# Softmax attention on transposed scores, with a pair of heads in one two-bank tile

## The chip, the core and the metric

The kernel runs on one core of a Trainium2 chip. A core has a matrix engine (PE, with its weight loads in PEld), a vector engine (DVE), a scalar engine for activations (ACT), a general engine (POOL) and a queue that only starts transfers (SP); each takes its instructions in the order of its own queue and waits on the others through semaphores. The metric is the device time of one execution, in microseconds (us), as the median over runs.

## What is computed

The program is two layers of a hybrid transformer on 512 latent and 256 context tokens of width 1024. In each layer a modulated norm and one input projection feed three mixers side by side: centred mean pooling (width 256), gated linear attention (width 256) and softmax attention (width 512). Their outputs are concatenated, projected, added to the residual, and followed by a squared-ReLU MLP. Layer 0 carries both streams; layer 1 carries the latents, and the context only as keys and values. The softmax attention has 8 query heads of 64 channels on 2 key heads:

```python
def gqa_attend(qb, k, v):
    s = jnp.einsum('bqhgd,bkhd->bhgqk', qb, k, preferred_element_type=jnp.float32) * HEAD_DIM ** -0.5
    p = jax.nn.softmax(s, axis=-1)
    return jnp.einsum('bhgqk,bkhd->bqhgd', p.astype(v.dtype), v)
```

A latent query sees 256 context keys and 512 latent keys in one softmax; a context query, in layer 0 only, sees the 256 context keys.

## The kernel before

Activations are kept feature-major (128 features by tokens). A product in single precision is made of passes over a rounded high part and a low rest (names ending in `hi`/`h` and `lo`/`l`); value products, transposes and sums run in full single precision, which PE does as two instructions each.

Per layer the emission goes: first norm and input projection; then the mixing half, in which four generators are advanced one step at a time by the letters of a string (`STEPS`, one for each layer: `g` gated linear attention, `a` the other projections, `m` modulation of later parts, `t` softmax attention, which itself advances `pool_thread`, the pooling mixer); then the output projection (`op`, L291 called from L1087 on) and the MLP. A scheduler then sets the order of each engine's queue from the emitted program. The string is the same in both kernels.

The softmax attention before, by names and lines:

- `k_stack` (L929 to L941) transposes the keys and writes `kh` and `kl`, each with the 64 channels twice, on both halves of the 128 rows.
- `q_stack` (L1022) transposes a pair of heads' queries and stacks high part over low part, `qs`, so that `kh`·`qs` and `kl`·`qs` over 128 rows give a score (L974, L975).
- A unit is a pair of heads and two query tiles of 128; layer 0 has 12 units (the third of each pair is for the context queries, L958 to L966), layer 1 has 8. `softmax_part` writes scores with queries on the rows (`sc`, 128 x 768), takes the row maximum on DVE (L977), and the exponential with its row sum on ACT (L978).
- `value_part` transposes the probabilities tile by tile (four 128 x 128 transposes for each key tile, L992), copies them out (L996 on ACT, L998 on DVE), multiplies by the values with the two heads side by side on the two column halves of PE (L1001), and brings the reciprocal sums, spread over the 64 rows of each head, in by another product (L1008), a copy and two operations (L1012 to L1017). The result goes to `mixh` and `mixl`, the operands of the output projection.

A unit's value part is emitted between the softmax steps of the unit after it. The banks of the accumulation memory are three pools: `psA` (2 tiles of two banks), `psB` (3 of one bank) and `psC` (1). Weight tiles land in `raw` (3 buffers) and are split into `hi` and `lo` (5 each); attention borrows buffers of all three kinds for `p` and `pe`.

## Time and profile before

| what | us |
| --- | --- |
| median of three runs | 1725.98 |
| lowest and highest run | 1724.35, 1727.54 |
| span of the profiled execution (its own total time isn't listed; the median is 6.1 more than the span) | 1719.9 |
| layer 0: keys' copies begin, out-projection begins | 223.3, 387.97 |
| layer 1: keys' copies begin, out-projection begins | 1179.8, 1302.18 |
| PE busy over the span | 1639.1 (95%) |
| DVE, ACT, POOL busy over the span | 866.9, 656.9, 480.3 |

The softmax attention lies in two stretches, about 224 to 387 us and 1180 to 1302 us, where it shares the engines with the gated linear attention and the pooling. The rest of the span is dominated by PE's weight products. Rows of the trace are quoted with their line, engine, operation and tile names; durations in rows are in us unless given as mean ns. PE's matmuls overlap, so what one costs PE is read from the distance between the starts of two rows.

### The profile page before, as it was taken

How to read it: one execution, taken by the hardware profiler on the slowest of the kernel's cores; microseconds unless marked ns; L12 is line 12 of the kernel's file. 1: busy time of each engine (PE TensorE's matmuls, PEld its weight loads, DVE VectorE, ACT ScalarE, POOL GpSimd, SP SyncE). 2: the span in 40 equal slices, each digit the busy share in tenths (PEclk: the TensorE clock that was granted, in tenths of full speed). 3: DMA queues.
4: the chain of work that ended last, by engine and by line, in shares of the span. 5: the costliest groups of instructions: out<-in, count | busy, mean ns of one | idle time of the engine just before them, and what ended most of it. 6: DMA issues, size and time to landing. Idle time of an engine off the chain costs nothing.

```text
span 1719.9 us, 28685 instructions
## 1 busy us (share of the span) xinstructions
PE 1639.1 (95%) x12059; PEld 1337.3 (78%) x12059; DVE 866.9 (50%) x1209; ACT 656.9 (38%) x1136; POOL 480.3 (28%) x514
## 2 busy tenths in 40 slices
...
GB/s 309 131 85 75 136 161 3 100 27 122 111 138 96 153 50 184 120 94 147 50 122 56 68 89 75 72 2 2 2 74 130 79 99 98 99 98 98 98 98 49
DMA packets 140256, 163.38 MB, mean 95 GB/s; under 512 B 9412, under 2 KB 116304, under 8 KB 140128
## 3 DMA queue, kind: packets, MB, share of 16 engines
...
q14 instruction: 34, 0.28, 0.0%
...
## 4 chain that ended last, share of the span: by engine, by line
PE 85%; DVE 5%; POOL 3%; DMA 2%; ACT 2%; issue 2%; SPq 0%; ACTq 0%; POOLq 0%; DVEq 0%
PE dn L291 25%; PE up L272 19%; PE op L291 7%; PE tm L291 6%; PE up L274 5%; PE fm L272 4%; PE av L1001 3%; PE pT L992 2%; PE pm L175 2%; PE up L281 2%; PE fm L274 2%; DMA rawm<-in_w_mod_dram 1%; PE sc L974 1%; PE att L722 1%; PE sc L975 1%
## 5 line engine op out<-in xcount | busy, mean ns | idle before, releaser
L144 ACT ACTIVATE whi<-raw 128x1024 fp32r<-128x1024 f32 (+2 forms) x182 | 184.8, 1031 | 582.2 <-PE dn L291 310.3
L1131 POOL TENSOR_TENSOR X<-X,rtmp 128x512 f32<-128x512 f32 x158 | 218.0, 1384 | 660.9 <-DVE rtmp L1130 660.6
L68 DVE TENSOR_TENSOR wlo<-raw,whi 128x1024 fp32r<-128x1024 f32 (+2 forms) x182 | 225.5, 1247 | 279.0 <-ACT whi L144 273.7
L291 PE MATMUL dn<-whi,ah 128*128 128x512 f32 x640 | 249.8, 390 | 0.4 <-DVE rtmp L1130 0.4
L291 PE MATMUL dn<-whi,al 128*128 128x512 f32 x640 | 249.1, 389 | 0.0
L291 PE MATMUL dn<-wlo,ah 128*128 128x512 f32 x640 | 246.8, 389 | 0.0
L1130 DVE TENSOR_TENSOR rtmp<-dn,ga 128x512 f32<-128x512 f32 x160 | 109.2, 689 | 231.4 <-PE dn L291 229.8
L272 PE MATMUL up<-h2h,whi 128*128 128x512 f32 x464 | 183.8, 396 | 0.7 <-ACT relu L1173 0.7
L272 PE MATMUL up<-h2l,whi 128*128 128x512 f32 x464 | 182.5, 393 | 0.0
L272 PE MATMUL up<-h2h,wlo 128*128 128x512 f32 x464 | 182.5, 393 | 0.0
L291 PEld LDWEIGHTS dn<-whi,ah 128*128 128x128 f32 x640 | 120.1, 188 | 29.8 <-ACT whi L144 4.2
L291 PEld LDWEIGHTS dn<-wlo,ah 128*128 128x128 f32 x640 | 120.1, 188 | 25.0
L291 PEld LDWEIGHTS dn<-whi,al 128*128 128x128 f32 x640 | 120.1, 188 | 24.5
L272 PEld LDWEIGHTS up<-h2h,whi 128*128 128x128 f32 x464 | 87.1, 188 | 31.4 <-ACT relu L1173 7.6
L272 PEld LDWEIGHTS up<-h2l,whi 128*128 128x128 f32 x464 | 87.1, 188 | 21.1 <-issue 1.7
L291 PE MATMUL tm<-whi,hTh 128*128 128x256 f32 (+1 forms) x352 | 102.6, 292 | 0.0
L272 PEld LDWEIGHTS up<-h2h,wlo 128*128 128x128 f32 x464 | 87.1, 188 | 19.6
L291 PE MATMUL tm<-whi,hTl 128*128 128x256 f32 (+1 forms) x352 | 101.3, 288 | 0.0
L291 PE MATMUL tm<-wlo,hTh 128*128 128x256 f32 (+1 forms) x352 | 100.5, 287 | 0.0
L291 PE MATMUL op<-whi,mixh 128*128 128x256 f32 x320 | 91.2, 285 | 0.9 <-ACT whi L144 0.9
L291 PE MATMUL op<-wlo,mixh 128*128 128x256 f32 x320 | 90.2, 284 | 0.3 <-DVE wlo L68 0.3
L291 PE MATMUL op<-whi,mixl 128*128 128x256 f32 x320 | 90.5, 283 | 0.0
...
## 6 DMA issues: line engine op xcount, KB each, us to landing
...
```

Source lines behind the costliest of these rows:

```text
L68: V.tensor_tensor(lo, full, hi.bitcast(F32), ALU.subtract)
L144: A.activation(hi, raw, AF.Copy)
L175: T.matmul(pm[32 * j:32 * j + 32, :], sstat[:, k, :], raw[:, (j % 2) * 512:(j % 2) * 512 + 512], start=(k == 0), stop=(k == KT - 1), skip_ ...
L272: T.matmul(ps[:, 0:NL], a, b[:, 0:NL], start=st, stop=sp_)
L274: T.matmul(ps[:, NL:NT], a, b[:, NL:NT], start=st, stop=sp_)
L281: T.matmul(ps[:, cs], a, b[:, cs], start=(k == 0 and i == 0), stop=(k == nk - 1 and i == 2))
L291: T.matmul(ps, a[:, sl], bb, start=(k == 0 and i == 0), stop=(k == nk - 1 and i == 2))
L722: T.matmul(ps[g * bw:(g + 1) * bw, o0:o0 + bw], xk[rows, j0:j0 + bw], xq[rows, i0:i0 + bw], start=True, stop=True)
L992: T.transpose(pt_[:, i * 128:(i + 1) * 128], p_[:, ki * 128:(ki + 1) * 128], ident)
L1001: T.matmul(av_[64 * hh:64 * hh + 64, 0:256], vst, pe[:, hh * 256:hh * 256 + 256], start=(ki == 0), stop=(ki == len(kts) - 1))
L1130: V.tensor_tensor(tmp, ps, ga[0 if t < 4 else 1][:, sl], ALU.mult)
L1131: (V if b == NB - 1 and not both and t == 3 else G).tensor_tensor(X[t][:, sl], X[t][:, sl], tmp, ALU.add)
```

## The change

The scores are made with the keys on the rows, `sT` (128 keys by 2 heads x 512 queries, two banks), so that the exponential, one instruction of 128 x 1024 for each key tile and pair, yields the operand of the value product directly: the transposes, the copies and the per-query row sums go away. A maximum along the rows no longer exists in this layout, so it is found ahead: `max_part` makes approximate scores of the pair with the queries on the rows (only the product with `kh`; 64 rows for the latent keys), reduces them on DVE to one maximum per query and head, transposes the maxima by a product with an identity, and writes the negated maximum into row 64 of the second query operand `qm`, against a row of ones in row 64 of `kl`. The score's second product then subtracts it. Sums over the keys are made by adding probability tiles (three adds on POOL, two on DVE, for each pair) and one product with ones. `weigh` turns sums into reciprocals by logarithm, exponential and one correction step on DVE. The buffers of the sums, `acc`, are of the `raw` kind. The context queries (`ctx_part`, layer 0) go the same way with 256 columns. `att_thread` emits a pair's values with the maximum of the next pair between them, and two steps of the pooling mixer after each pair.

Lines above the attention move by 5 to 6; L291 becomes L296. The core of the diff:

```diff
     ident = const.tile([128, 128], F32, name="ident")
     make_identity(nc, ident)
+    identr = const.tile([128, 128], F32R, name="identr")
+    V.tensor_copy(identr, ident)
+
+    nmx = const.tile([128, 6, 33], F32R, name="nmx")
+    A.activation(nmx, ident[:, 0:1].unsqueeze(1).to_broadcast([128, 6, 33]), AF.Copy, scale=0.0)
     mhalf = const.tile([128, 1], F32, name="mhalf")
...
@@ -937,129 +943,153 @@
                 A.activation(kh[0:64], src, AF.Copy)
                 sub_lo(kl[0:64], src, kh[0:64])
                 A.activation(kh[64:128], src, AF.Copy)
-                G.tensor_copy(kl[64:128], kl[0:64].bitcast(F32))
+                A.activation(kl[64:65], ident[64:65, 64:65].to_broadcast([1, NT]), AF.Copy)
                 kst.append((kh, kl))
...
-        def q_stack(hp):
+        def max_part(hp):
             mix_new(4 + hp)
             pq = [psB("qT"), psB("qT")] if both else [psB("qT")]
             for t in live:
                 T.transpose(pq[t // 4][:, (t % 4) * 128:(t % 4 + 1) * 128], qview(t, hp), ident)
             for hh in range(2):
-                qs = slot("qs", F32R)
+                qs, qm = slot("qs", F32R), slot("qm", F32R)
+                hr, lr = slice(64 * hh, 64 * hh + 64), slice(64 - 64 * hh, 128 - 64 * hh)
                 for i, pq_ in enumerate(pq):
                     n0, n1 = (0, NL) if i == 0 else (NL, NT)
-                    src = pq_[64 * hh:64 * hh + 64, 0:n1 - n0]
-                    A.activation(qs[0:64, n0:n1], src, AF.Copy)
-                    sub_lo(qs[64:128, n0:n1], src, qs[0:64, n0:n1])
-                qst[hp * 2 + hh] = qs
+                    src = pq_[hr, 0:n1 - n0]
+                    A.activation(qs[hr, n0:n1], src, AF.Copy)
+                    sub_lo(qs[lr, n0:n1], src, qs[hr, n0:n1])
+                G.tensor_copy(qm[0:64, 0:N_], qs[hr, 0:N_].bitcast(F32))
+                qst[2 * hp + hh] = (qs, qm)
+            yield
+            kh = kst[hp // 2][0]
+            parts = mp.tile([128, 2, 6, 2], F32, tag="mxp", name=nm("mxp"), bufs=1)
+            for t in live:
+                ts_ = slice(t * 128, (t + 1) * 128)
+                ps = psB("mxc")
+                for hh in range(2):
+                    T.matmul(ps[:, hh * NC:(hh + 1) * NC], qst[2 * hp + hh][0][:, ts_], kh[:, NL:NT], start=True, stop=True)
+                if t < 4:
+                    pl_ = [psB("mx"), psB("mx")]
+                    for hh in range(2):
+                        hr = slice(64 * hh, 64 * hh + 64)
+                        T.matmul(pl_[hh], qst[2 * hp + hh][0][hr, ts_], kh[hr, 0:NL], start=True, stop=True)
+                V.tensor_reduce(parts[:, 1, t], ps.rearrange("p (h k) -> p h k", h=2), AX.X, ALU.max, negate=True)
+                if t < 4:
+                    for hh in range(2):
+                        V.tensor_reduce(parts[:, 0, t, hh:hh + 1], pl_[hh], AX.X, ALU.max, negate=True)
+                yield
+            V.tensor_tensor(nmx[:, 0:4, 0:33:32], parts[:, 0, 0:4], parts[:, 1, 0:4], ALU.min)
+            if both:
+                V.tensor_copy(nmx[:, 4:6, 0:33:32], parts[:, 1, 4:6])
+            ps = psA("mT")
+            for t in live:
+                T.matmul(ps[0:33, t * 128:(t + 1) * 128], nmx[:, t], identr, start=True, stop=True)
+            for hh in range(2):
+                r0 = 32 * hh
+                A.activation(qst[2 * hp + hh][1][64:65, 0:N_], ps[r0:r0 + 1, 0:N_], AF.Copy)
+            yield
+        def scores(ps, hp, hh, kt, q0, qn):
+            kh, kl = kst[hp // 2]
+            qs, qm = qst[2 * hp + hh]
+            ks = slice(kt * 128, (kt + 1) * 128)
+            T.matmul(ps, kh[:, ks], qs[:, q0:q0 + qn], start=True, stop=False)
+            T.matmul(ps, kl[0:65, ks], qm[0:65, q0:q0 + qn], start=False, stop=True)
+        def weigh(hp, av, acc, q0, n):
+            f = slot("f", w=512)[:, 0:n]
+            A.activation(f, av, AF.Copy)
+            sm = psB("sum")[:, 0:n]
+            for hh in range(2):
+                T.matmul(sm[64 * hh:64 * hh + 64], one.to_broadcast([128, 64]), acc[hh], start=True, stop=True)
+            r, u = slot("r", w=512)[:, 0:n], slot("u", w=512)[:, 0:n]
+            A.activation(r, sm, AF.Ln)
+            A.activation(r, r, AF.Exp, scale=-1.0)
+            V.scalar_tensor_tensor(u, r, -1.0, sm, ALU.mult, ALU.mult)
+            V.tensor_tensor(r, f, r, ALU.mult)
+            V.scalar_tensor_tensor(r, u, 2.0, r, ALU.add, ALU.mult)
+            mhi, mlo = mixT[4 + hp]
+            A.activation(mhi[:, q0:q0 + n], r, AF.Copy)
+            G.tensor_tensor(mlo[:, q0:q0 + n], r, mhi[:, q0:q0 + n].bitcast(F32), ALU.subtract)
+        def lat_part(hp):
+            av = psC("av")
+            P = []
+            def values(kt):
+                for hh in range(2):
+                    T.matmul(av[64 * hh:64 * hh + 64, :], vview(kt, hp // 2), P[kt][:, hh * 512:hh * 512 + 512],
+                             start=(kt == 0), stop=(kt == 5))
+            for kt in range(6):
+                s_ = psA("sT")
+                for hh in range(2):
+                    scores(s_[:, hh * 512:hh * 512 + 512], hp, hh, kt, 0, NL)
+                P.append(wp.tile([128, 1024], F32, tag="lo" if kt % 2 else "hi", name=nm("p")))
+                A.activation(P[kt], s_, AF.Exp)
+                if kt:
+                    values(kt - 1)
+                if kt == 1:
+                    acc = wp.tile([128, 1024], F32, tag="raw", name=nm("acc"), bufs=3)
+                    G.tensor_tensor(acc, P[0], P[1], ALU.add)
+                elif kt in (2, 3):
+                    G.tensor_tensor(acc, acc, P[kt], ALU.add)
+                yield
+            values(5)
+            acc2 = wp.tile([128, 1024], F32, tag="raw", name=nm("acc"), bufs=3)
+            V.tensor_tensor(acc2, P[4], P[5], ALU.add)
+            V.tensor_tensor(acc, acc, acc2, ALU.add)
+            yield
+            weigh(hp, av, [acc[:, 0:512], acc[:, 512:1024]], 0, NL)
+            yield
+        def ctx_part(hp):
+            av = psC("avc")[:, 0:NC]
+            s_ = psA("sTc")
+            for hh in range(2):
+                for i in range(2):
+                    o = i * 512 + hh * NC
+                    scores(s_[:, o:o + NC], hp, hh, 4 + i, NL, NC)
+            p_ = wp.tile([128, 1024], F32, tag="hi", name=nm("p"))
+            A.activation(p_, s_, AF.Exp)
+            yield
+            for i in range(2):
+                for hh in range(2):
+                    o = i * 512 + hh * NC
+                    T.matmul(av[64 * hh:64 * hh + 64, :], vview(4 + i, hp // 2), p_[:, o:o + NC],
+                             start=(i == 0), stop=(i == 1))
+            acc = slot("accx", w=512)
+            G.tensor_tensor(acc, p_[:, 0:512], p_[:, 512:1024], ALU.add)
+            yield
+            weigh(hp, av, [acc[:, 0:NC], acc[:, NC:512]], NL, NC)
+            yield
         def att_thread():
             k_stack()
             yield
-            q_stack(0)
-            yield
-            nonlocal nunits
-            units = [(hp, q0) for hp in range(4) for q0 in ((0, 2, 4) if both else (0, 2))]
-            nunits = len(units)
-            prev = iter(())
-            for n, (hp, q0) in enumerate(units):
-                P = []
-                for i, _ in enumerate(softmax_part(n, hp, q0, P)):
-                    for _ in range(2 if i < 2 else 1):
-                        next(prev, None)
+            yield from max_part(0)
+            for hp in range(4):
+                nxt = max_part(hp + 1) if hp < 3 else iter(())
+                for part in (lat_part(hp), ctx_part(hp) if both else iter(())):
+                    for _ in part:
+                        next(nxt, None)
+                        yield
+                for _ in nxt:
                     yield
-                run(prev)
-                if q0 == 0 and hp < 3:
-                    q_stack(hp + 1)
-                prev = value_part(n, hp, q0, P)
                 next(pool_, None)
-                yield
-            yield from prev
+                next(pool_, None)
             run(pool_)
```

How the queues stand now, at three places. Numbers at the end of a name tell tiles apart.

ACT in layer 0, where the queries of the third pair are copied: `qT` are the transposed queries, `qs` their stacked copies, `p` the probabilities of the second pair. Before:

```order
L1016 ACTIVATE mixh_2671<-f_3388 128x256
L1016 ACTIVATE mixh_2671<-f_3501 128x256
L1033 ACTIVATE qs_3629<-qT_3621 64x512
L1033 ACTIVATE qs_3629<-qT_3622 64x256
L978 ACTIVATE p_3404,sm_3401<-sc_3489,nmx_3402 128x768
L1033 ACTIVATE qs_3634<-qT_3621 64x512
L1033 ACTIVATE qs_3634<-qT_3622 64x256
L978 ACTIVATE p_3405,sm_3401<-sc_3506,nmx_3402 128x768
```

After:

```order
L1037 ACTIVATE p_3627<-sT_3622 128x1024
L964 ACTIVATE qs_3547<-qT_3539 64x512
L964 ACTIVATE qs_3547<-qT_3540 64x256
L1037 ACTIVATE p_3647<-sT_3642 128x1024
L964 ACTIVATE qs_3554<-qT_3539 64x512
L964 ACTIVATE qs_3554<-qT_3540 64x256
L1037 ACTIVATE p_3712<-sT_3707 128x1024
L1037 ACTIVATE p_3731<-sT_3726 128x1024
```

The copies stood among the four exponentials of the first of the second pair's three units, with two more units to come before the third pair's scores; they now stand between the third and the fifth of the second pair's six exponentials. On PE, the third pair's approximate scores (`mxc`, `mx`, which read those `qs`) stand among the second pair's last scores and values (`av`):

```order
L975 MATMUL mxc_3573<-kh_2669,qs_3547 128x256
L1029 MATMUL av_3529<-p_3647,UV_1141 64x512 x2
L1002 MATMUL sT_3726<-qs_2902,kh_2663 128x512
L1003 MATMUL sT_3726<-qm_2903,kl_2664 128x512
L1002 MATMUL sT_3726<-qs_2909,kh_2663 128x512
L1003 MATMUL sT_3726<-qm_2910,kl_2664 128x512
L975 MATMUL mxc_3573<-kh_2669,qs_3554 128x256
L980 MATMUL mx_3576<-kh_2669,qs_3547 128x512
L1029 MATMUL av_3529<-p_3712,UV_1141 64x512 x2
L980 MATMUL mx_3577<-kh_2669,qs_3554 128x512
```

PE in layer 1, around the second half of the pooling mixer (`pool`, from `pm`) before:

```order
L974 MATMUL sc_12049<-kh_11209,qs_11348 128x512
L975 MATMUL sc_12049<-kl_11210,qs_11348 128x512
L974 MATMUL sc_12049<-kh_11209,qs_11348 128x256
L975 MATMUL sc_12049<-kl_11210,qs_11348 128x256
L920 MATMUL pool_12114<-pm_11200,wpl_9588 128x512
L974 MATMUL sc_12125<-kh_11215,qs_11923 128x512
L975 MATMUL sc_12125<-kl_11216,qs_11923 128x512
```

After:

```order
L1011 MATMUL sum_11724<-acc_11514,one 64x512 x2
L957 MATMUL qT_11769<-ident,Uq_10498 128x128 x3
L957 MATMUL qT_11769<-ident,Uq_10725 128x128
L925 MATMUL pool_11754<-pm_10900,wpl_9288 128x512
L1002 MATMUL sT_11760<-qs_11450,kh_10915 128x512
L1003 MATMUL sT_11760<-qm_11451,kl_10916 128x512
L1002 MATMUL sT_11760<-qs_11455,kh_10915 128x512
L1003 MATMUL sT_11760<-qm_11456,kl_10916 128x512
L1002 MATMUL sT_11784<-qs_11450,kh_10915 128x512
```

The pooling product stood between the scores of two units of softmax attention; it now stands ahead of the third pair's first scores, behind the sums (`sum`) of the second pair.

PE in layer 0, where attention ends. Before:

```order
L992 MATMUL pT_4434<-ident,pcx_4371 128x128 x2
L992 MATMUL pT_4434<-ident,pcx_4372 128x128 x2
L1008 MATMUL rb_4443<-ident,sm_4340 64x128 x4
L1001 MATMUL av_4424<-pe_4430,UV_1137 64x256 x2
L1001 MATMUL av_4424<-pe_4439,UV_1137 64x256 x2
L291 MATMUL op_4480<-whi_4470,mixh_3393 128x256
L291 MATMUL op_4480<-whi_4470,mixl_3394 128x256
```

After:

```order
L1002 MATMUL sTc_4122<-qs_3854,kh_2669 128x256
L1003 MATMUL sTc_4122<-qm_3855,kl_2670 128x256
L1002 MATMUL sTc_4122<-qs_3854,kh_2669 128x256
L1003 MATMUL sTc_4122<-qm_3855,kl_2670 128x256
L1011 MATMUL sum_4109<-acc_4062,one 64x512 x2
L1067 MATMUL avc_4121<-p_4131,UV_1141 64x256 x4
L296 MATMUL op_4348<-whi_4338,mixh_3805 128x256
L296 MATMUL op_4348<-whi_4338,mixl_3806 128x256
```

The last row sets of attention were the value products of the context unit (`pcx`); they are now the sums of the last pair and its context values (`avc`). The first output projection in the new queue reads the weight tile `whi_4338`, whose transfer into a `raw` buffer is the third of four on SP's queue for that projection.

70 lines of the change are left out of this document (removed).

## The prediction

> **What bounds the kernel now.** I read the page's list of engines and its chain first, then a view of the two stretches with softmax attention, then single rows there.
>
> ```profile
> PE 1639.1 (95%) x12059; PEld 1337.3 (78%) x12059; DVE 866.9 (50%) x1209; ACT 656.9 (38%) x1136; POOL 480.3 (28%) x514
> PE 85%; DVE 5%; POOL 3%; DMA 2%; ACT 2%; issue 2%; SPq 0%; ACTq 0%; POOLq 0%; DVEq 0%
> core 0: us, PE busy (x) PEld busy (x) DVE busy (x) ACT busy (x) POOL busy (x), PEclk, DMA share, GB/s
> 224.00:386.70 162.70, 145.39 (x1740) 95.97 (x1735) 103.77 (x169) 102.07 (x230) 55.29 (x74) 0.96 0.18 63
> 1180.00:1302.20 122.20, 108.77 (x1215) 73.24 (x1213) 82.72 (x131) 81.83 (x174) 38.83 (x55) 0.94 0.12 44
> 262.00:290.00 28.00, 21.91 (x500) 15.40 (x500) 24.96 (x38) 17.28 (x40) 17.04 (x25) 0.88 0.01 3
> 1186.00:1215.00 29.00, 23.34 (x341) 16.31 (x341) 26.31 (x40) 22.40 (x52) 22.29 (x33) 0.82 0.01 2
> 320.00:387.00 67.00, 63.54 (x470) 41.96 (x469) 35.35 (x58) 44.95 (x107) 12.54 (x19) 1.00 0.22 81
> ```
>
> PE is the bound over the whole, and the change touches only the 163 and 122 us of the two stretches; what comes behind them keeps its order and its time. Inside, two regimes: at the start of each stretch DVE is busy for 24.96 of 28 and 26.31 of 29 us and PE has holes, towards the end PE is busy for 63.54 of 67. Work taken from PE pays only in the second regime; work given to DVE costs in the first.
>
> **What the change does to each engine.** The distances between starts give what a piece costs PE:
>
> ```profile
> 325.87 1.08 PE L1001 MATMUL av<-pe,UV 128*64 128x256 f32 x8
> 326.88 0.66 PE L992 MATMUL pT<-ident,p 128*128 128x128 f32 x4
> 327.47 0.65 PE L1001 MATMUL av<-pe,UV 128*64 128x256 f32 x4
> 328.06 0.66 PE L992 MATMUL pT<-ident,p 128*128 128x128 f32 x4
> 331.45 0.47 PE L974 MATMUL sc<-kh,qs 128*128 128x512 f32 x1
> 331.77 0.39 PE L975 MATMUL sc<-kl,qs 128*128 128x512 f32 x1
> 331.99 0.28 PE L974 MATMUL sc<-kh,qs 128*128 128x256 f32 x1
> 332.11 0.28 PE L975 MATMUL sc<-kl,qs 128*128 128x256 f32 x1
> 332.23 0.38 PE L992 MATMUL pT<-ident,pcx 128*128 128x128 f32 x2
> ```
>
> Four transposes take 0.59 (326.88 to 327.47), a key tile's four value instructions 0.59, eight in a row 1.01; so 0.43 for four more without a switch. A score instruction of 512 columns takes 0.22, or 0.32 behind full-precision work, one of 256 takes 0.12. A pair in layer 0 costs before: scores 8 x 0.78 = 6.2 and 1.0 for the context, transposes 14 x 0.59 = 8.3, values 14 x 0.58 = 8.1, sums about 1.3: 24.9. After: scores 24 x 0.22 + 6 x 0.1 = 5.9 and 1.1, approximate scores 8 x 0.22 + 12 x 0.12 = 3.2, transposed maxima about 0.7, values 6 x 1.0 + 1.2 = 7.2 (512 columns: 0.86 and a switch of 0.15), sums 1.6: 19.7. Layer 1 by the same prices: 20.9 and 16.4. PE saves 4 x 5.2 + 4 x 4.5 = 39.
>
> ```profile
> L977 DVE TENSOR_REDUCE nmx<-sc 128x1 f32<-128x768 f32 x64 | 60.5, 953 | 25.9 <-PE sc L975 25.5
> L962 DVE TENSOR_REDUCE nmx<-scc 128x4 f32<-128x1024 f32 x4 | 4.9, 1223 | 2.0 <-PE scc L961 1.9
> L978 ACT ACTIVATE p<-sc,nmx 128x768 f32<-128x768 f32 x64 | 57.5, 899 | 18.7 <-DVE nmx L977 18.1
> L1173 ACT ACTIVATE relu<-up 128x768 f32<-128x768 f32 x32 | 25.6, 800 | 71.6 <-PE up L274 55.6 <-DMA brow<-in_b_mod_dram 14.4 <-PE up L281 1.6
> L1173 ACT ACTIVATE relu<-up 128x512 f32<-128x512 f32 x32 | 18.6, 581 | 0.0
> L68 DVE TENSOR_TENSOR wlo<-raw,whi 128x1024 fp32r<-128x1024 f32 x170 | 213.9, 1266 | 273.5 <-ACT whi L144 268.5 <-PE pm L175 2.3 <-ACT pe L996 1.9
> L1131 POOL TENSOR_TENSOR X<-X,rtmp 128x512 f32<-128x512 f32 x158 | 218.0, 1384 | 660.9 <-DVE rtmp L1130 660.6
> L699 DVE TENSOR_TENSOR xq<-xq,gq 128x768 f32<-128x768 f32 x14 | 16.8, 1209 | 0.8 <-ACT xq L698 0.7
> L1130 DVE TENSOR_TENSOR rtmp<-dn,ga 128x512 f32<-128x512 f32 x160 | 109.2, 689 | 231.4 <-PE dn L291 229.8
> L68 DVE TENSOR_TENSOR qs<-qT,qs 64x512 fp32r<-64x512 f32 x16 | 11.0, 690 | 2.9 <-ACT qs L1033 2.3
> L1014 DVE TENSOR_TENSOR f<-av,f 128x256 f32<-128x256 f32 x20 | 8.4, 418 | 12.1 <-ACT pe L996 6.1 <-PE av L1001 5.3 <-ACT f L1012 0.6
> L1017 POOL TENSOR_TENSOR mixl<-f,mixh 128x256 fp32r<-128x256 f32 x20 | 16.5, 823 | 115.6 <-ACT mixh L1016 115.5
> L913 POOL TENSOR_TENSOR pl<-pl,edge 64x8 f32<-64x8 f32 x12 | 5.2, 436 | 19.7 <-DVE pl L910 12.1 <-DVE pl L905 3.1 <-DVE pl L907 2.9
> L915 DVE SCALAR_TENSOR_TENSOR pm<-pl,invw,pl 64x512 f32<-64x512 f32 x8 | 6.1, 758 | 0.4 <-POOL pl L914 0.3
> ```
>
> A reduction of 512 columns is not in the trace; 1.223 - 0.953 for 256 columns gives 0.953 - 0.27 = 0.69 (bounds 0.61, half the largest row, and 0.953). An exponential of 1024 columns is 0.899 and the 0.22 that 256 columns cost between the two L1173 rows, 1.12 (bounds 1.02, by those rows alone, and 1.20, by the 768 row in proportion). An add of 128 x 1024 is 1.27 on DVE (the `wlo` row) and 2 x 1.384 = 2.77 on POOL. So DVE has per pair in layer 0: 14 reductions 9.7, adds 2.5, corrections 3 x 0.69 + 3 x 0.42 = 3.3, query rests 2 x (0.69 + 0.42) = 2.2, together 17.7, 71 over the layer. Before, a pair has 8 x 0.953, 1.2, the same rests, four copies of about 0.69 and three products of 0.418, 15.0 and some small ones, about 63 over the layer. POOL gains three adds, 8.3, a context add of 1.4 and two casts, about 11 per pair. ACT loses the copies and most row sums. No engine then fills its stretch: PE 145 - 21 = 124 of 163, DVE 112, POOL about 100.
>
> **The chain that sets the end.** With no engine full, the order of the queues decides. Call m0 to m3 the times at which DVE has a pair's maxima; scores of a pair wait for them, since the negated maximum rides in their second product. What the queue order (shown with the change) makes of it, link by link:
>
> ```profile
> L937 ACT ACTIVATE kh<-kT x4: 803/805/807, 223.3 to 1182.4; 64x768 fp32r<-64x768 f32 x4
> L782 PE MATMUL rg<-ident,rsg x80: 272/273/476, 247.9 to 1255.0; 128*64 128x128 f32 x80
> L920 PE MATMUL pool<-pm,wpl 128*128 128x512 f32 x8 | 4.5, 628 | 0.4 <-issue 0.2 <-DVE dg L735 0.2
> 381.82 3.76 DMA raw<-in_w_out_dram
> 385.60 1.06 ACT whi L144
> 386.69 1.24 DVE wlo L68
> 387.97 7.10 PE op L291 x57
> 1302.18 2.59 PE op L291 x20
> ```
>
> Layer 0. The first approximate scores stand on PE behind the product `rg`, which ran from 247.9, so DVE begins about 250; ahead of m0 it has 13 reductions (9.0), nine products of gated attention like the L699 row (9 x 1.25 = 11.3) and a copy or two: m0 = 271. To m1: DVE 13 reductions, four products, query rests, masks and two `qe` products, about 21, PE about 27 with the gated attention's small products: +26. To m2: adds 2.5, sums 1, logarithm, exponential and context exponential 3, context scores and values with small products about 6; then six key tiles at 2.0 on PE (scores 1.0, values 1.0), 12; the third pair's query copies stand on ACT behind the third and fourth of these exponentials, so 11 of 14 reductions come after, 7.6, with adds, gated attention's scaling and its wait, 5: +37 (31 to 43, by how much of the last 12 overlaps the tiles). To m3 the same without the small products: 5.5 + 12 + 12.5 and about 2 of wait: +32. To the out-projection: 4.8 for the maxima's row, the context unit and a pooling product ahead of the tiles, 12 for these, adds and sum 5.3; then the transfer of the weight tile that its first rows read, which lands in a `raw` buffer that `acc` holds until the sum has read it, by the rows above 3.76 + 1.06: +27. 271 + 26 + 37 + 32 + 27 = 393 against 387.97: +5, range -1 to +11.
>
> Layer 1. Keys at 1180; DVE has 12 reductions (8.3), products and states, about 21: m0 = 1201. Then +25 and +23 by the same counts with four tiles. To m3: adds 2.5, sum and reciprocal 2.4, weighing 2.1; then the pooling chain, whose product the queue puts ahead of the third pair's first scores: a copy to `mixh` 0.6, POOL's rest (0.823 for 256 columns, about 1.4 here) and copy 0.8, four DVE rows of 0.69, POOL's four edge products of at most 0.436, 1.4, two rows of 0.758, the product 0.63, about 9 with the hand-offs; then 12 for tiles and about 8 for the reductions left over: +36 (33 to 39). PE has nothing to do in those 9. To the out-projection the maxima's row 1.7, tiles 12, the last exponential 1.1, adds 2.5 and the sum 0.5: +18. 1201 + 25 + 23 + 36 + 18 = 1303 against 1302.18: +1, range -4 to +8.
>
> Hand-offs between engines are left out so far. The rows at 385.60 to 387.97 show 0.03 and 0.04 for one, the L977 row shows 25.9 / 64 = 0.4; some 70 of them on the chain cost 2 to 28, and I take 0.1, 7. Total: +5 + 1 + 7 = +13. 1719.9 + 13 = 1733, and with the 6.1 by which the median stood over the span, **1739**. With the ends of the three terms, 1723 to 1773; all far ends together are unlikely, so its own range is 1726 to 1757.
>
> **A rule against the change.** POOL's adds read and write the same memory as DVE's. The `xq` row took 1.209 for 768 columns beside POOL's work, 1.57 ns a column, the `wlo` row 1.24. In the Trainium skill, "SBUF — State Buffer", section "SBUF: two separate sides", DVE with two operands from that memory and POOL exclude each other for a whole instruction. By that rule a DVE add or product could wait out one POOL add, 24 x 2.77 / 2 = 33 more by estimate, 1772. The trace's 1.57 against 1.24 is far less than a full exclusion, so it is not in my sum; the ratio itself is used in the last rival.
>
> **Rivals.**
>
> *Overlap works, PE stays the bound or DVE fills the stretch.* For it: 63.54 of 67 us busy at the end of layer 0, and the emission puts a pair's maxima between the tiles of the pair before. Against: the copies' place on ACT and the serial links above. All of PE's saving, -39, gives 1726 - 39 = 1687.
>
> *Only part overlaps.* If the reductions counted behind the tiles on the way to m2 and m3 in layer 0 and to m3 in layer 1, 8 each, hide beneath them: 1739 - 24 = 1715. For it: three banks in `psB` let PE run one reduction ahead. Against: those copies again, and adds of 2.77 on POOL ahead of the `qm` casts that the pair needs.
>
> *Stalls and saving cancel,* about 1726: the chain without hand-offs, -7, and with the low end of layer 0, -6.
>
> *Clock and shared memory make it slower still.* Where PE has holes the granted clock was 0.88 and 0.82, where it is dense 1.00. The change puts holes through both stretches: PE's 124 and 91 us there at 0.85 instead of 0.95 are 215 x 0.12 = 25 more, half of it on the chain, 13; POOL's 24 adds at the 1.57 / 1.24 ratio give 24 x 0.7 = 17, half on the chain, 8: 1739 + 21 = 1760. It decides from a mean clock below about 0.88 in both stretches. The Trainium skill, "TensorE: Matmul & The Clock Gate", section "Part 1: The HAM clock gate", says that the clock halves after an idle window of about 3.4 us; the hole of 9 us in layer 1 would do it, and the rows at 0.82 and 0.88 agree in direction.
>
> **How the numbers follow.** A measurement of this kernel tells 0.2%, 3.5 us, from no change. The chain as forecast, slower by 1730 to 1757: 0.42. Beyond 1757 by clock and memory: 0.08. Cancelled, 1722.5 to 1729.5: 0.12. Part overlap, 1702 to 1722: 0.22. Full overlap, 1675 to 1702: 0.16. So faster 0.38, same 0.12, slower 0.50. The range leaves out about 0.1 at each end: 1693 to 1758; the forecast's own range stands above.
>
> **What would show it.** Right: PE's busy time over both stretches together down by 35 to 40 with spans no shorter; PE waiting for `nmx`, `qm` or `pool` ahead of `sT`, 9 us at one place in layer 1; idle time of DVE's reductions ended by `mx` and `mxc` behind the tiles; out-projections starting near 393 to 400 and, from a layer-1 start that is as much later, 122 to 129 after the keys; a last transfer of `raw` on layer 0's chain. Wrong: reductions that run between the key tiles in all pairs, or an exponential or a 512-column value product well off 1.12 and 1.0, the two prices that the tile of 2.0 rests on. If PE's slots came out above 2.5 the saving itself would be gone.

## The result, and the profile after

| | before | after | forecast |
| --- | --- | --- | --- |
| median of the runs, us | 1725.88 | 1788.66 (1787.81 to 1789.55) | 1739 (1693 to 1758) |
| ratio to before, 95% interval | | 1.0382 (1.0361 to 1.0403) | 1.008 |
| span of the profiled execution | 1719.9 | 1787.0 | 1733 |
| layer 0, first copy of the keys to first out-projection | 163.4 | 194.0 | 170 |
| first out-projection to layer 1's keys | 793.1 | 800.2 | |
| layer 1, first copy of the keys to first out-projection | 122.3 | 148.2 | 123 |
| from there to the end | 417.8 | 421.5 | |

The change made the kernel 63 us slower. The direction was forecast, the size was not: the time lies outside the range. Of the span's 67.1 us, 30.6 lie in the stretch of layer 0, 25.9 in that of layer 1, and 10.8 behind the two, where no instruction had been changed. The profiled execution of the changed kernel lies 2.2 us under its own time (1787.0 of 1789.17), that of the kernel before 6.1 under its median, so it was probably some 4 us quicker than that median, and the spans differ by that much more than the medians, which are 62.8 apart.

The page of the changed kernel, its list of engines and the granted clock in 40 slices:

```profile
PE 1660.6 (93%) x11459; PEld 1311.7 (73%) x11459; DVE 904.3 (51%) x1238; ACT 631.7 (35%) x985; POOL 547.0 (31%) x546
PEclk9999877888999999999999999897788999999999
```

PE has 600 instructions fewer than before (11459 against 12059) and is busy for 21.5 us longer. The two stretches tell why. The windows view of the changed kernel (start and end, length, busy time and instructions of PE, PEld, DVE, ACT, POOL, then granted clock, DMA share, GB/s):

```profile
223.10:417.10 194.00, 159.10 (x1432) 82.55 (x1430) 134.18 (x189) 89.11 (x138) 89.60 (x90) 0.82 0.18 59
1217.30:1365.50 148.20, 112.66 (x932) 57.40 (x930) 86.06 (x136) 67.02 (x108) 68.42 (x69) 0.80 0.07 26
```

The clock fell from 0.96 and 0.94 to 0.82 and 0.80, and no engine is full: PE has 35 idle us in each stretch, DVE 60 and 62. This is the chain of hand-offs that was forecast, and longer than forecast. The same view, cut where DVE has finished the maxima of each pair (its row L986, 268.7 to 1346.6), that is at m0 to m3 and, in layer 0, at the out-projection:

```profile
223.10:268.70 45.60, 35.66 (x270) 18.71 (x268) 29.96 (x51) 18.24 (x30) 23.63 (x22) 0.76 0.36 114
268.70:297.30 28.60, 26.08 (x444) 14.43 (x446) 21.31 (x31) 15.05 (x26) 14.45 (x13) 0.67 0.01 2
297.30:347.40 50.10, 43.40 (x512) 25.10 (x510) 32.97 (x53) 21.11 (x37) 18.78 (x24) 0.88 0.03 6
347.40:385.60 38.20, 29.99 (x110) 14.06 (x108) 31.55 (x37) 16.21 (x24) 18.28 (x17) 0.81 0.26 104
385.60:417.10 31.50, 23.97 (x102) 10.25 (x98) 18.38 (x21) 18.49 (x24) 14.47 (x15) 0.93 0.20 61
1217.00:1237.10 20.10, 14.06 (x76) 8.03 (x74) 16.11 (x28) 9.93 (x15) 7.38 (x12) 0.65 0.00 1
1237.10:1268.40 31.30, 25.23 (x188) 13.02 (x188) 17.44 (x30) 16.96 (x33) 19.29 (x19) 0.83 0.00 1
1268.40:1302.80 34.40, 24.74 (x453) 14.11 (x454) 21.29 (x39) 14.56 (x26) 16.33 (x18) 0.77 0.01 2
1302.80:1346.60 43.80, 31.92 (x165) 15.54 (x163) 25.66 (x37) 15.21 (x22) 17.10 (x17) 0.88 0.09 35
```

The links against the forecast: layer 0 gave m0 = 268.7 (271), then +28.6 (+26), +50.1 (+37), +38.2 (+32), +31.5 (+27). Layer 1 gave +19.8 from the keys (+21), then +31.3 (+25), +34.4 (+23), +43.8 (+36), +18.9 (+18). Only two links lie within 2 us; the largest misses are m1 to m2 in both layers.

The prices of single instructions on ACT, DVE and POOL were not the cause. The groups of the changed kernel (busy us, mean ns of one, then the idle time ahead of them and what ended it):

```profile
L1037 ACT ACTIVATE p<-sT 128x1024 f32<-128x1024 f32 x48 | 48.9, 1023 | 37.7 <-PE sT L1003 37.5
L984 DVE TENSOR_REDUCE mxp<-mx 128x1 f32<-128x512 f32 x64 | 42.1, 681 | 6.4 <-PE mx L980 6.2
L981 DVE TENSOR_REDUCE mxp<-mxc 128x2 f32<-128x512 f32 x40 | 27.2, 682 | 12.9 <-PE mxc L975 12.9
L1044 POOL TENSOR_TENSOR acc<-acc,p 128x1024 f32<-128x1024 f32 x16 | 38.5, 2404 | 11.2 <-ACT p L1037 10.6
```

The exponential took 1.02 us (forecast 1.12), a reduction 0.68 (0.69), an add on POOL 2.40 (2.77). What failed is how they stand to each other.

**The third pair of layer 0,** with the fourth pair's maxima, shows the chain. On PE, from m2 at 347.4 (start, duration, line, operation and tiles; in brackets the idle time ahead and what ended it):

```profile
353.87 0.58 PE L1002 MATMUL sT<-qs,kh 128*128 128x512 f32 x1
...
374.11 0.58 PE L975 MATMUL mxc<-kh,qs 128*128 128x256 f32 x1 [5.10 <-DVE qs L68]
...
380.50 0.79 PE L980 MATMUL mx<-kh,qs 64*128 64x512 f32 x1 [0.46 <-DVE mxp L984]
```

First scores 6.5 us after m2, six key tiles until 369.0, then 5.1 us in which PE waits for the fourth pair's query rests, then all approximate scores in a row from 374.1, in step with DVE's reductions, until 385.6. Of the fourth pair's approximate scores, which had been emitted between the tiles, a single product (`mxc`, at 367.61) ran ahead of the last values. Over both layers 36 of the 104 reductions began between the first and the last exponential of some pair's six tiles. Six tiles with none of them there took 11.9 to 12.9 us from the first exponential to the last, those with eight to twelve of them 17.0 to 24.1. Products of the gated attention stand there as well, and six tiles with these and only two reductions took 17.3, so the reductions are not all of the difference. Why the rests were late stands on DVE:

```profile
362.81 2.87 DVE L910 TENSOR_TENSOR pl<-pl 128x526 f32<-128x526 f32 x1 [0.51 <-POOL pl L909]
...
366.87 0.68 DVE L68 TENSOR_TENSOR qs<-qT,qs 64x512 fp32r<-64x512 f32 x1
367.59 2.80 DVE L915 TENSOR_TENSOR pl<-pl 128x520 f32<-128x520 f32 x1
```

and beside it on POOL:

```profile
362.75 2.37 POOL L1044 TENSOR_TENSOR acc<-acc,p 128x1024 f32<-128x1024 f32 x1
...
367.49 2.34 POOL L1044 TENSOR_TENSOR acc<-acc,p 128x1024 f32<-128x1024 f32 x1
```

A pooling add of 526 columns, which takes 0.71 at this place when POOL has no such add (e1, below), took 2.87: it started 0.06 us behind POOL's add and ended 0.56 after it. L915 repeats this: it ended 0.56 after an add that had started 0.10 earlier. By these lengths the pooling mixer and the query rests behind it lost some 4 us here.

**From m1 to m2 in layer 0** another chain stands among the maxima, the scaling of the gated attention (`ss`, `rsg`, `rg`):

```profile
309.42 0.50 PE L1002 MATMUL sT<-qs,kh 128*128 128x512 f32 x1
...
331.04 0.50 PE L980 MATMUL mx<-kh,qs 64*128 64x512 f32 x1
331.47 0.51 PE L975 MATMUL mxc<-kh,qs 128*128 128x256 f32 x2
331.90 1.08 PE L1029 MATMUL av<-p,UV 128*64 128x512 f32 x4
...
337.09 2.72 PE L776 MATMUL ss<-blk,o 128*128 128x2 f32 x12
341.30 2.83 PE L787 MATMUL rg<-ident,rsg 128*64 128x128 f32 x24 [1.50 <-DVE rsg L223]
344.06 0.80 PE L975 MATMUL mxc<-kh,qs 128*128 128x256 f32 x2
```

Between 337.09 and 344.06 no approximate score runs. The same 24 `rg` took 1.53 in the kernel before:

```profile
314.84 1.53 PE L782 MATMUL rg<-ident,rsg 128*64 128x128 f32 x24
```

**In layer 1** three waits stand out on PE:

```profile
1268.60 1.97 PE L1011 MATMUL sum<-acc,one 128*64 128x512 f32 x4 [4.09 <-DVE nmx L986]
...
1283.58 2.05 PE L925 MATMUL pool<-pm,wpl 128*128 128x512 f32 x2 [8.74 <-DVE pm L920]
...
1321.61 2.04 PE L925 MATMUL pool<-pm,wpl 128*128 128x512 f32 x2 [10.61 <-DVE pm L920]
```

The last was in the forecast, with 9; the one of 8.74, the first half of the pooling mixer ahead of the second pair's first scores, was not.

**Behind the stretch** of layer 0 the first out-projections run at a low clock:

```profile
417.12 0.39 PE L296 MATMUL op<-whi,mixh 128*128 128x256 f32 x1 [1.87 <-ACT whi L149]
...
419.62 0.41 PE L296 MATMUL op<-whi,mixh 128*128 128x256 f32 x1
419.83 0.41 PE L296 MATMUL op<-whi,mixl 128*128 128x256 f32 x1
...
426.01 0.28 PE L296 MATMUL op<-whi,mixh 128*128 128x256 f32 x1
426.13 0.28 PE L296 MATMUL op<-whi,mixl 128*128 128x256 f32 x1
```

From start to start 0.21, and 0.12 from 424.3 on; about 3.5 us are lost, at work that the change does not touch.

### The profile page after: what moved, and what is told of

It reads as the page before. It is cut to its first block, busy times and chain, and to the rows that moved or that the text cites. A ratio compares the mean times of both kernels' runs of the same rounds, so it can differ in the third digit from the quotient of the medians.

```text
span 1787.0 us, 27365 instructions
## 1 busy us (share of the span) xinstructions
PE 1660.6 (93%) x11459; PEld 1311.7 (73%) x11459; DVE 904.3 (51%) x1238; ACT 631.7 (35%) x985; POOL 547.0 (31%) x546
## 5 line engine op out<-in xcount | busy, mean ns | idle before, releaser
L296 PE MATMUL dn<-whi,ah 128*128 128x512 f32 x640 | 249.8, 390 | 0.4 <-DVE rtmp L1160 0.4
L296 PE MATMUL dn<-whi,al 128*128 128x512 f32 x640 | 249.1, 389 | 0.0
L296 PE MATMUL dn<-wlo,ah 128*128 128x512 f32 x640 | 246.8, 389 | 0.0
L1160 DVE TENSOR_TENSOR rtmp<-dn,ga 128x512 f32<-128x512 f32 x160 | 109.1, 688 | 232.7 <-PE dn L296 231.9
L296 PEld LDWEIGHTS dn<-whi,ah 128*128 128x128 f32 x640 | 120.1, 188 | 29.8 <-ACT whi L149 4.2
L296 PEld LDWEIGHTS dn<-wlo,ah 128*128 128x128 f32 x640 | 120.1, 188 | 25.0
L296 PEld LDWEIGHTS dn<-whi,al 128*128 128x128 f32 x640 | 120.2, 188 | 24.5
L277 PEld LDWEIGHTS up<-h2h,whi 128*128 128x128 f32 x464 | 87.1, 188 | 31.5 <-ACT relu L1203 7.6
L296 PE MATMUL tm<-whi,hTh 128*128 128x256 f32 (+1 forms) x352 | 102.5, 291 | 1.2 <-DVE st L677 1.2
L296 PE MATMUL tm<-whi,hTl 128*128 128x256 f32 (+1 forms) x352 | 101.2, 288 | 0.0
L296 PE MATMUL tm<-wlo,hTh 128*128 128x256 f32 (+1 forms) x352 | 100.4, 287 | 0.0
L296 PE MATMUL op<-whi,mixh 128*128 128x256 f32 x320 | 93.2, 293 | 6.1 <-ACT whi L149 4.7
L296 PE MATMUL op<-wlo,mixh 128*128 128x256 f32 x320 | 91.8, 290 | 0.5 <-DVE wlo L68 0.5
L296 PE MATMUL op<-whi,mixl 128*128 128x256 f32 x320 | 92.0, 288 | 0.0
```

The lines of the kernel that those rows point to most:

```text
L277: T.matmul(ps[:, 0:NL], a, b[:, 0:NL], start=st, stop=sp_)
L296: T.matmul(ps, a[:, sl], bb, start=(k == 0 and i == 0), stop=(k == nk - 1 and i == 2))
L1160: V.tensor_tensor(tmp, ps, ga[0 if t < 4 else 1][:, sl], ALU.mult)
```

## The experiments

The stretches run from the first copy of the keys to the first out-projection; "sum" adds the two layers. Kernels that share a row of "before" ran beside it.

| kernel | median | ratio to before (95%) | layer 0 | layer 1 | sum |
| --- | --- | --- | --- | --- | --- |
| before | 1725.88 | | 163.4 | 122.3 | 285.7 |
| after | 1788.66 | 1.0382 (1.0361 to 1.0403) | 194.0 | 148.2 | 342.2 |
| before | 1723.84 | | | | |
| e1_no_pool_adds | 1776.33 | 1.0298 (1.0269 to 1.0327) | 183.4 | 151.8 | 335.2 |
| e2_no_max | 1736.80 | 1.0081 (1.0062 to 1.0101) | 165.4 | 125.1 | 290.5 |
| e3_pooling_ahead | 1797.62 | 1.0427 (1.0403 to 1.0451) | 202.4 | 151.5 | 353.9 |
| e4_fill | 1812.28 | 1.0522 (1.0502 to 1.0543) | 216.8 | 150.5 | 367.3 |
| before | 1722.84 | | | | |
| e5_maxima_pair_ahead | 1816.03 | 1.0537 (1.0518 to 1.0556) | 200.0 | 169.2 | 369.2 |
| e6_acc_own | 1793.71 | 1.0406 (1.0386 to 1.0426) | 195.7 | 147.3 | 343.0 |
| e7_gla_first | 1836.15 | 1.0663 (1.0636 to 1.0691) | 152.5 | 129.4 | 281.9 |
| e8_maxima_and_pooling_spread | 1790.72 | 1.0391 (1.0347 to 1.0434) | 204.1 | 148.8 | 352.9 |
| before | 1722.22 | | | | |
| e9_adds_on_dve | 1789.11 | 1.0395 (1.0373 to 1.0416) | 191.0 | 152.4 | 343.4 |
| e10_queries_ahead | 1784.36 | 1.0365 (1.0342 to 1.0388) | 190.5 | 151.8 | 342.3 |
| e11_queries_ahead_adds_on_dve | 1780.85 | 1.0360 (1.0327 to 1.0392) | 183.2 | 149.1 | 332.3 |
| e12_all_three | 1773.43 | 1.0305 (1.0284 to 1.0326) | 192.6 | 140.7 | 333.3 |
| before | 1721.61 | | | | |
| e13_before_gla_first | 1759.10 | 1.0218 (1.0187 to 1.0248) | 116.5 | 96.1 | 212.6 |
| e14_no_max_gla_first | 1765.09 | 1.0252 (1.0222 to 1.0283) | 117.2 | 99.1 | 216.3 |
| e15_no_max_no_pool_adds | 1710.96 | 0.9940 (0.9917 to 0.9963) | 150.0 | 118.0 | 268.0 |
| e16_banks_for_maxima | 1804.45 | 1.0477 (1.0443 to 1.0511) | 208.1 | 152.9 | 361.0 |

### What the maxima, POOL's adds and the clock cost in place

**e2** removes the approximate scores and their reductions; the maxima's row stays, with zeros.

```diff
-                ps = psB("mxc")
...
-                V.tensor_reduce(parts[:, 1, t], ps.rearrange("p (h k) -> p h k", h=2), AX.X, ALU.max, negate=True)
...
-                A.activation(P[kt], s_, AF.Exp)
+                A.activation(P[kt], s_, AF.Exp, scale=1.0 / 1024)
```

> The changed kernel without the approximate scores and the reductions: nothing is found and zero is subtracted (the exponential's argument is scaled down to stay finite), the rest stays. Theory Q: what waited for the maxima in series goes, about 9 us ahead of the first pair and 8 to 12 for two or three pairs of each layer, 60 to 90 us less, about 1700 to 1730, and PE's holes with it. Theory C: the same, since a dense PE gets its clock back, granted clock near 0.98 as before; PE then is the bound and the time goes to 1690 or below. Theory L: POOL's adds still hold DVE, but DVE has little left to do, 20 us less at most, 1768.

The maxima are 51.7 us of the two stretches (342.2 to 290.5), and 3.0 of the 3.8 points. What is left is still no faster than before (1.0081). The windows of this kernel over its two stretches:

```profile
224.70:390.10 165.40, 120.88 (x1352) 61.69 (x1350) 99.39 (x125) 87.26 (x138) 94.96 (x90) 0.87 0.21 70
1188.90:1314.00 125.10, 88.36 (x869) 44.66 (x867) 65.91 (x84) 66.01 (x109) 69.51 (x69) 0.81 0.08 30
```

PE is busy for 45 us less than before (209 against 254) in stretches that are not shorter: without the maxima it has 81 us of idle time, and no other engine is full either. One of the waits, on PE and then on ACT:

```profile
359.16 1.97 PE L1051 MATMUL avc<-p,UV 128*64 128x256 f32 x8 [6.91 <-ACT f L992]
```

```profile
357.28 0.80 ACT L978 ACTIVATE qm<-mT 1x768 fp32r<-1x768 f32 x1
358.11 0.38 ACT L964 ACTIVATE qs<-qT 64x256 fp32r<-64x256 f32 x1
358.51 0.60 ACT L992 ACTIVATE f<-av 128x512 f32<-128x512 f32 x1
```

The accumulator of the values has one bank; the context's values wait for its copy `f`, and this stands on ACT behind the next pair's query copies and its row of maxima.

**e1** adds up three of the six key tiles only, so that POOL has no such adds.

```diff
-                if kt == 1:
-                    acc = wp.tile([128, 1024], F32, tag="raw", name=nm("acc"), bufs=3)
-                    G.tensor_tensor(acc, P[0], P[1], ALU.add)
-                elif kt in (2, 3):
-                    G.tensor_tensor(acc, acc, P[kt], ALU.add)
```

> The changed kernel (1788.66 us) without POOL's three adds of probabilities for each pair: the latents' sums are taken over three of the six key tiles, with the two adds on DVE kept, so the weights come out too large. Theory Q (links of the queues in series, PE waits for maxima and for the pooling product): POOL's adds are beside the chain, 3 to 6 us less, about 1783 to 1786. Theory L (POOL's adds hold up DVE's operations with two operands): DVE's operations in layer 0 lose about 20 us of overlength, 15 to 25 us less, about 1764 to 1774. Theory C (the granted clock of PE): as Q, clock unchanged near 0.95.

0.8 of the 3.8 points: layer 0 is 10.6 us shorter, layer 1 is 3.6 longer, and 5.2 are won behind the stretches. With as many instructions as in the changed kernel (326 against 325 in the two stretches) DVE is busy there for some 20 us less (116.6 and 83.9 us against 134.2 and 86.1). The DVE row that had taken 2.87 beside a POOL add is back at its own length, at the same place of the program:

```profile
357.93 0.71 DVE L910 TENSOR_TENSOR pl<-pl 128x526 f32<-128x526 f32 x1 [0.50 <-POOL pl L909]
```

The edit also takes POOL's adds out of the chain that leads to the sums, so what it gains is what both effects cost together.

**e15** removes both, so its sums cover three key tiles and its maxima are zero.

```diff
-                ps = psB("mxc")
...
-                    G.tensor_tensor(acc, P[0], P[1], ALU.add)
```

> The changed kernel, in its own order, without approximate scores and reductions and also without POOL's three adds for each pair (sums over three of six key tiles). Without the maxima alone it stood at 1736.8 us, 1.008 of before, with some 46 us less of PE's time in the two stretches. If the sums by POOL are what eats the saving there: 15 to 30 us less, 1707 to 1722, at last below before. If the gated attention's own chain and the pooling steps set the time: within 8 us of 1736.8.

POOL's adds are worth 7.0 us of the stretches where the maxima are there (e1) and 22.5 where they are not (290.5 to 268.0): the two delays lie partly on top of each other. With both gone the kernel is 0.6% faster than before, 17.7 us in the stretches, of which 5 are lost again behind them (77.4 us from the first out-projection to the MLP in layer 0, 72.4 before). So the new layout, with two things missing that it needs, earns about a quarter of the 39 us that PE was to save.

**e4** repeats each approximate score three times and puts 24 products ahead of each pooling product, so that PE has shorter holes.

```diff
+                for _ in range(24):
+                    T.matmul(ps[:, 0:NL], kst[0][0][:, 0:128], kst[0][0][:, 0:NL], start=True, stop=True)
...
-                    T.matmul(ps[:, hh * NC:(hh + 1) * NC], qst[2 * hp + hh][0][:, ts_], kh[:, NL:NT], start=True, stop=True)
+                    for _ in range(3):
+                        T.matmul(ps[:, hh * NC:(hh + 1) * NC], qst[2 * hp + hh][0][:, ts_], kh[:, NL:NT], start=True, stop=True)
```

> The changed kernel with useless matmuls in places where PE waits: each approximate score is made three times into the same bank, and 24 of 512 columns stand ahead of each pooling product; about 60 us of PE work at full clock that nobody reads. Theory C: the granted clock in the two stretches goes from about 0.8 to above 0.9 and the time falls by 10 us or more in spite of the added work. Theory Q: PE's holes are filled but the chain stays, 1788 to 1800. Theory L: as Q.

```profile
225.50:442.20 216.70, 184.20 (x1640) 107.95 (x1638) 134.10 (x191) 88.89 (x138) 90.35 (x90) 0.90 0.15 53
1239.80:1390.30 150.50, 134.23 (x1109) 79.20 (x1107) 87.97 (x136) 67.15 (x108) 68.65 (x69) 0.91 0.07 25
```

The filler did raise the clock, from 0.82 and 0.80 to 0.90 and 0.91, and the kernel became slower by another 1.4 points. In layer 1 PE was busy for 21.6 us more and the stretch grew by 2.3; in layer 0, 25.1 more and 22.8 longer. The higher clock did not shorten the chain here. What the low clock costs cannot be read from this kernel, since the filler stands in the same queue as the links.

The repeats tell one thing more, what an approximate score costs in a row of its own kind (granted clock 1.00):

```profile
348.31 0.96 PE L984 MATMUL mx<-kh,qs 64*128 64x512 f32 x3 [0.33 <-DVE mxp L988]
349.19 0.98 PE L978 MATMUL mxc<-kh,qs 128*128 128x256 f32 x6
```

Three products of 512 columns over 64 rows take 0.88 from start to start of the two rows, where a single one took 0.43 in the changed kernel (331.04 to 331.47): a further one costs 0.23. Of the six of 256 columns the first start is at 349.19, the next ones at 349.41, 349.53, 349.65, 349.77 and 349.89, and the following product of another shape starts at 350.10: 0.12 within the row, and 0.1 more at its beginning and at its end.

### The attention by itself

**e7** and **e13** move all steps of the gated attention ahead of the softmax attention, in the changed kernel and in the one before, by the same strings; **e14** is e7 without the maxima (as e2).

```diff
-STEPS = ("aggaamgmagagaaagaaaamgaaaaamagaaaagaaaaaagmgaaaagamggmggmgtt"
-         "mggtttmtttgttgtmgtggtttgtttgttmgtmtgttmgtt",
-         "ggggagaggaaagaaggaaaaaagaaaagaaaggaagaaggatatgatttttgaatgttg"
-         "tttgggtttgttggttttgtttgt")
+STEPS = ("aggaamgmagagaaagaaaamgaaaaamagaaaagaaaaaagmgaaaagamggmggmgmggmggmgggggmgmgmgtttttttttttttttttttttttttt",
+         "ggggagaggaaagaaggaaaaaagaaaagaaaggaagaaggaagagaaggggggggggtttttttttttttttttttttttttt")
```

> The changed kernel with the emission string reordered: all remaining steps of the gated linear attention ahead of the steps of the softmax attention. Theory Q with the gated attention's links (scaling of its output 8 us between the second pair's maxima in layer 0, masks and products of its levels) as a large part: 10 to 20 us less. If the gated attention's work was cover for the softmax attention's waits, it is slower, by 5 to 20 us.

> The kernel before with the same reordered emission string: all remaining steps of the gated linear attention ahead of the softmax attention, so that the old softmax attention runs alone with the pooling. The changed kernel with that order has stretches of 152.5 and 129.4 us from the keys' copies to the out-projection. If the new softmax attention is slower by itself: the old one takes what its PE work takes, 102 and 86 us with the key and query transposes, 105 to 120 and 90 to 105. If it is slower only by what it does to the gated attention: 145 to 160 and 120 to 135.

> The changed kernel with that order and without approximate scores and reductions (zero is subtracted, the exponential's argument scaled down). PE's work for it is about 66 and 54 us by the prediction's prices. If the maxima in series are what the new attention loses by itself, 52 us over both layers or more go: 152.5 to about 115 to 125, 129.4 to 95 to 105, still well above PE's work, because of the remaining links (sums over POOL, weighing, pooling). If those links are hidden: 75 to 90 and 60 to 75.

The windows of the three over their stretches, e13 (the attention before), e7 (the changed one), e14 (the changed one without maxima):

```profile
290.10:406.60 116.50, 103.73 (x727) 70.72 (x727) 75.34 (x116) 79.43 (x183) 22.05 (x45) 0.94 0.12 43
1242.00:1338.10 96.10, 85.73 (x585) 58.41 (x585) 62.31 (x87) 64.11 (x128) 14.75 (x26) 0.93 0.15 53
```

```profile
287.60:440.10 152.50, 116.92 (x415) 57.37 (x415) 98.65 (x133) 64.18 (x91) 60.19 (x61) 0.78 0.10 37
1284.00:1413.40 129.40, 95.62 (x305) 43.29 (x305) 63.95 (x92) 48.42 (x63) 45.35 (x40) 0.79 0.07 28
```

```profile
288.60:405.80 117.20, 84.25 (x325) 38.76 (x325) 58.60 (x71) 63.87 (x91) 59.65 (x61) 0.82 0.14 50
1243.90:1343.00 99.10, 67.62 (x232) 28.55 (x232) 33.30 (x40) 48.42 (x63) 45.96 (x40) 0.79 0.09 37
```

Three readings. The gated attention is not the cause: alone but for the pooling mixer, the changed attention is 69.3 us longer than the old one (281.9 against 212.6), in place 56.5. Nearly the whole work of the maxima comes out as time: without them the stretches are 65.6 us shorter, while DVE is busy for 70.7 us less and PE for 60.7, so next to nothing of it was covered by other work. Whether DVE's reductions or PE's approximate scores set the pace is not told by these two kernels. And without maxima the changed attention is as long as the old one (216.3 and 212.6), though PE is busy for 37.6 us less (151.9 against 189.5): PE is idle for 64 us of it and no other engine is full (ACT 112 us, POOL 106). What is left to set its length is the chain of a pair, from scores over exponentials, values, sums and the copy `f` to the next pair; its links were not taken out one by one. The old one, by contrast, has its maxima in those 212.6.

### Other orders and other places

**e3** draws the pooling mixer's steps ahead, between the first pair's maxima.

```diff
-            yield from max_part(0)
+            for _ in max_part(0):
+                next(pool_, None)
+                yield
...
-                next(pool_, None)
-                next(pool_, None)
```

> The changed kernel with all steps of the pooling mixer emitted beside the first pair's maxima and none between the pairs. Theory Q: the holes of PE ahead of the second and third pair's scores in layer 1 (11.7 us each, ended by the pooling product) and the smaller ones in layer 0 go, while the first pair's maxima get some 6 us of DVE more for each layer: 12 to 20 us less, 1769 to 1777. Theory L: no change, within 4 us. Theory C: the part of Q that PE waits, and a clock a little higher, 0.96.

Slower by 0.45 points. The later hole closed (m2 to m3 in layer 1 takes 29.0 instead of 43.8 us), but m1 comes 27 us later in layer 0 and 19 in layer 1: the same chain stands at another place.

**e5** finds the maxima a whole pair earlier.

```diff
             yield from max_part(0)
+            yield from max_part(1)
             for hp in range(4):
-                nxt = max_part(hp + 1) if hp < 3 else iter(())
+                nxt = max_part(hp + 2) if hp < 2 else iter(())
```

> The changed kernel with query copies and maxima emitted one pair further ahead: those of pairs 0 and 1 before the first scores, those of pair hp+2 between the key tiles of pair hp. Theory Q (links in series between DVE's maxima and PE's tiles): the last two pairs of each layer no longer wait for maxima, 8 to 12 us for each of three of them, while the second pair's 9 us come ahead of the first scores: 10 to 25 us less, 1764 to 1779. If instead the sum of work on DVE, POOL and PE in the first half of each stretch decides, the time stays within 5 us of 1788.66.

Slower by 1.5 points, the slowest of these orders. The waits have moved, not gone; on PE in layer 0:

```profile
345.53 7.91 PE L1029 MATMUL av<-p,UV 128*64 128x512 f32 x24 [7.56 <-ACT f L1008]
362.45 0.58 PE L975 MATMUL mxc<-kh,qs 128*128 128x256 f32 x1 [7.77 <-DVE qs L68]
```

PE now waits for the copy `f`, as in e2, and then still for the query rests.

**e8** is e5 with the pooling steps spread between the tiles.

```diff
+            yield from max_part(1)
...
-                    for _ in part:
+                    for i, _ in enumerate(part):
                         next(nxt, None)
+                        if i in (1, 4):
+                            next(pool_, None)
```

> As the kernel with maxima a pair ahead, and with the steps of the pooling mixer emitted between the second and third and the fifth and sixth key tile of each pair instead of between the pairs. Theory Q: the two holes of 11.7 us in layer 1 go too, 10 to 20 us less than with the maxima ahead alone, 1745 to 1769. If the place of the pooling steps is as good as any other, as the slower run with all of them ahead would suggest, no change against the maxima ahead alone.

1.5 points better than e5, by layer 1 (169.2 to 148.8); not to be told from the changed kernel, and its runs lie as far apart as 1781.6 and 1800.1.

**e6** gives the sums buffers of the kinds `hi` and `lo`, so that no weight tile waits for a `raw` buffer.

```diff
-                    acc = wp.tile([128, 1024], F32, tag="raw", name=nm("acc"), bufs=3)
+                    acc = wp.tile([128, 1024], F32, tag="hi", name=nm("acc"))
...
-            acc2 = wp.tile([128, 1024], F32, tag="raw", name=nm("acc"), bufs=3)
+            acc2 = wp.tile([128, 1024], F32, tag="lo", name=nm("acc"))
```

> The changed kernel with the buffers of the sums taken from the kinds of the probabilities instead of the weights' landing buffers. In the changed kernel the output projection of layer 0 takes 77.8 us from its first product to the MLP's first, 72.4 before, and begins after a late transfer. If those buffers are the cause: 5 to 9 us less, 1780 to 1784, and the 72 us back. If PE's granted clock there is the cause (0.85 in its first 23 us), no change.

No gain, and from the first out-projection to the MLP still 77 us in layer 0. The `raw` buffer was not what delayed the projections. The low clock is not all of it either: in this kernel the granted clock of these 77 us was 1.00, while PE waited for 2.5 us of them and ran 1.6 us of the attention's own products there.

**e9** puts POOL's adds on DVE.

```diff
-                    G.tensor_tensor(acc, P[0], P[1], ALU.add)
+                    V.tensor_tensor(acc, P[0], P[1], ALU.add)
                 elif kt in (2, 3):
-                    G.tensor_tensor(acc, acc, P[kt], ALU.add)
+                    V.tensor_tensor(acc, acc, P[kt], ALU.add)
```

> The changed kernel with the three adds of each pair moved from POOL to DVE; the result is complete. DVE gets 24 adds of 1.23 us, 30 us, more. Theory L (in the changed kernel DVE's operations with two operands stretch to 1.5 to 2.9 us where a POOL add of 2.4 us runs beside them): those lengths go back to 0.4 to 1.2 and the time falls in spite of the added work, 5 to 15 us less, 1774 to 1784. If the stretched operations are a coincidence, DVE's 30 us more make it slower by 10 to 25 us.

Within the interval of the changed kernel: DVE takes on 24 adds of about 1.23, 30 us, and is rid of the waits beside POOL's: its busy time in the stretches grows by 11.7 us only (220.2 to 231.9).

**e10** takes the copies of the queries two pairs ahead; **e11** is e10 and e9; **e12** is e11 with the pooling steps spread as in e8.

```diff
-            yield from max_part(0)
+            mps = [max_part(i) for i in range(4)]
+            next(mps[0])
+            next(mps[1])
+            yield
+            yield from mps[0]
...
+                        if i == 0 and j == 1 and hp < 2:
+                            next(mps[hp + 2])
+                        if i == 0 and j in (1, 4):
+                            next(pool_, None)
```

(The last two lines are e12's alone.)

> The changed kernel with only the query copies emitted a pair earlier (transposes, high part, rest and the cast on POOL), the maxima where they were. In the changed kernel the third pair's reductions of layer 0 wait 5.1 us for a query rest on DVE and then run in series for 11.5 us behind the second pair's values. If the copies are what keeps the maxima behind the values: reductions between the tiles in three pairs of each layer, 15 to 30 us less, 1759 to 1774. If something else does (the three banks that maxima, sums and transposes share, or DVE's queue), no change within 6 us.

> Both edits together: query copies a pair earlier and the adds on DVE. If the two causes are separate, the sum of both gains; 1745 to 1765 if both hold, and between the two single kernels if one of them holds no gain.

> Query copies a pair earlier, adds on DVE, and the pooling steps between the second and third and the fifth and sixth key tile of a pair. The pooling product ahead of a pair's first scores made PE wait 11.7 us twice in layer 1; moving all pooling ahead cost 9 us, moving it between the tiles beside maxima ahead gained 25. Expected 10 to 20 us below the kernel with two edits, about 1735 to 1755; still not faster than before.

Early queries alone change nothing that can be told. With the adds on DVE as well the stretches come to 332.3, 10 less than after, though the ratio's interval still meets that of the changed kernel; with the pooling spread layer 1 gets to 140.7. e12 is the fastest complete version of the new layout, 1773.4, and still 3.05% slower than before; its layer 0 is 9.4 us longer than that of e11. None of the three came down to the times that the hoped-for gains would have given (1774, 1765 and 1755). In layer 1 of e12 all 36 reductions of the later three pairs do begin between the exponentials of the pair before, but the six tiles then take 33, 26 and 22 us from the first exponential to the last, where the last pair's, with no reduction among them, take 14. Standing between the tiles is not yet being covered by them; what the pooling steps and the gated attention add there was not separated.

**e16** is e11 with the transposed queries and the sums in `psA`, so that the three banks of `psB` serve the approximate scores alone.

```diff
-            pq = [psB("qT"), psB("qT")] if both else [psB("qT")]
+            pq = [psA("qT"), psA("qT")] if both else [psA("qT")]
...
-            sm = psB("sum")[:, 0:n]
+            sm = psA("sum")[:, 0:n]
```

> Queries ahead and adds on DVE as before, and the sums and the transposed queries in the two-bank tiles, so that the three single banks serve the maxima alone. If the turn that maxima, sums and query transposes take in these three banks holds the maxima behind the values: 10 to 25 us below the 1780.85 of the kernel without this edit. If DVE's own work decides: within 6 us of it.

24 us slower than e11. Here the transposed queries and the sums take their turn in the two tiles of the scores' pool, which may be the reason; it was not followed further.

No complete version beat the kernel before, so none was carried on.

## Why the prediction was right and wrong

**Right: the direction and its mechanism.** PE stopped being the bound and the order of the queues took over. The maxima ran in a row behind the tiles (374.1 to 385.6), PE waited for query rests and for `pool`, and e2 and e7 against e14 show that the maxima are the bulk of it. The two prices on which a tile rested held, and where nothing stood between the tiles a slot came out at 2.14 instead of 2.0: scores 0.34 + 0.24 + 0.23 + 0.32 from start to start, values 1.01; 48 tiles make 7 us of that. The 12 for six tiles held as well for the pairs without reductions among them (11.9 to 12.9).

**Wrong: the size, by 54 us of the span** (67.1 against 13), or 50 of the median, since the 6.1 that I added for its distance from the span came out as 2.2. Layer 0 ended 24 us later than forecast (417.1 against 393), layer 1 took 25 more (148.2 against 123.2), and 10.8 came up behind the stretches where 7 were set aside for all hand-offs together; the rest is that the first row of the out-projection before stood at 386.7, not at 387.97. What I had forecast for the two stretches together, 293, is about what they take with no maxima at all (290.5, e2). The steps that failed:

1. *"Far less than a full exclusion, so it is not in my sum."* The rule that I left out, of the Trainium skill, "SBUF — State Buffer", section "SBUF: two separate sides" (DVE with two operands from that memory and POOL exclude each other for a whole instruction), is what the trace shows: 2.87 beside POOL's 2.37, 0.71 in e1 without it. My counter-evidence was a mean ratio, 1.57 to 1.24 ns a column, over rows of which only some met POOL at work, and POOL's instructions in the rows quoted were of 0.8 to 1.4 us; such a mean can't tell an exclusion from a slower port. DVE's busy time in the stretches holds some 20 us of such waits (e1), where the estimate had 33, and the adds cost the stretches 7.0 us (e1), or 22.5 where the maxima are missing (e15 against e2). So this term is a small part of the 54. The last rival had 17 for it by the mean ratio, with 8 of them on the chain: near the measured sizes, but by luck, since it took the port to be slower.

2. *m1 to m2 in layer 0, +37.* The 7.0 us of `ss`, `rsg` and `rg` stand between the maxima, at the low clock and with the rest of the maxima queued behind them; I had 5 for the adds, the scaling and its wait. The tiles, which I let run in 12, took 22.5 from the first score to the last values (309.4 to 331.9); 5.2 of that are the gated attention's own products (315.3 to 320.6), and sums, transposes, the first approximate scores and waits stand among them too.

3. *Layer 1, +25 and +23.* I put one pooling hole into the sum, 9, and overlooked that `att_thread` draws two pooling steps after each pair: the first half waits ahead of the second pair's first scores in the same way, 8.74. That is the larger part of the 11 us by which m1 to m2 was longer; what made m0 to m1 longer by 6 was not followed. The copied order of PE's queue showed the one place; the same question for the other pair was not asked.

4. *Work behind the stretches at no cost.* The start of layer 0's out-projection runs at the low clock for about 7 us and loses 3.5; layer 1's starts at full clock, then waits for 2.8 us on ACT's copies of weights and runs at half clock for 3.4 (1373.2 to 1376.7). The time from the out-projection to the next layer grew by 7.1, and to the end by 3.7. I took the clock as a rival with a chance of 0.08. Its condition, a mean clock under 0.88 in both stretches, was met (0.82, 0.80), and of the rivals it is the one on whose side the time lies, though its 1760 is still 29 short. The Trainium skill, "TensorE: Matmul & The Clock Gate", section "Part 1: The HAM clock gate", names an idle window of some 3.4 us; the trace agrees where PE waited for 5.10 us (the rows behind it take 0.79 instead of 0.50), but the slow stretch at 417 follows idle times of at most 1.87 us over the 28 us ahead, so holes much shorter than the window are no safety.

5. *PE's saving of 39.* It was never tested at full clock, and its busy time rose by 18 over the stretches (254 to 272) where I wanted 35 to 40 less as a sign that I was right: a sign that the granted clock can turn round is no test. One of its prices was wrong in any case. An approximate score of 512 columns took 0.43 (331.04 to 331.47) instead of 0.22, one of 256 took 0.21 (331.47 to 331.90 for two) instead of 0.12. By these rows a pair's maxima in layer 0 cost 4 x (2 x 0.43 + 2 x 0.21) + 4 x 0.21 = 6.0, not 3.2, unless two heads' products run side by side, as 10 of the 32 such pairs did. That alone takes up to half of the saving, before any wait. The repeats of e4 show the term that I had left out: the product itself costs the 0.23 and 0.12 of my prices, and the rest is 0.1 on either side of each change from one shape of product to another, which I had counted for the values (as 0.15) but not for the approximate scores.

The deeper error is common to 1 to 3: I added up a chain from busy times, as if the other work on each queue stood aside, and then took 0.1 us for a hand-off. Eight of the ten links came out longer, by 1 to 13 us. The three rivals on the fast side, with 0.50 together, all needed cover for the maxima or for the tiles behind them, and e7 against e14 finds next to none. That PE would be idle for long was in the forecast; that a layout whose PE work is 45 us lighter would be no faster even without its maxima (e2) was not.

**What stays open.** How the remaining chain of a pair (e14) divides among the exponentials, POOL's sums, the copy `f` and the pooling mixer; whether DVE's reductions or PE's approximate scores set the pace of the maxima; what the low clock by itself costs inside the stretches; and why e16 is slower.
